# A streaming-encoder step on one core: the down projection's token operands of the fifth pair on are stored and loaded as high and low parts

## The chip, the cores and the metric

One core of one Trainium2 chip runs the whole step as one program. The time is device microseconds (us) of one execution. Five engines work side by side, each on its own instructions in order: TensorE (PE in the profile, with its weight loads listed as PEld), VectorE (DVE), ScalarE (ACT), GpSimd (POOL) and SyncE (SP), whose only work here is to issue the DMAs.

## The reference

The step is one layer of an encoder on 512 prompt frames with 16 meta tokens, and 64 frames of a running stream. After attention comes a SwiGLU feed-forward stage, in which the change lies:

```
h = rmsnorm(x, lp['norm_ffn_g'])
x = x + (jax.nn.silu(h @ lp['ffn_w_gate']) * (h @ lp['ffn_w_up'])) @ lp['ffn_w_down']
...
y_prompt = rmsnorm(xp[:, N_META:], final_norm_g)
y_sample = rmsnorm(xs, final_norm_g)
```

The model width is 2048, `D_FF` is 5632, and 576 tokens pass through this stage. Everything is float32, with an accuracy that one reduced-precision pass does not give.

## The kernel before

**Split operands.** TensorE multiplies in the format fp32r. To keep float32's accuracy each operand is split into a high part (a ScalarE copy into fp32r) and a low part (a VectorE subtraction, source minus high part), and a product is three matmuls: high by high, low by high, high by low. Weights' parts are `wh` and `wl`; the token operands' parts are `bh` and `bl` (pool `bc`).

**Winograd products.** The feed-forward matrices are multiplied in 2 by 2 block form with seven products instead of eight (`winograd`, line 1065). A token operand is one of four quarters (feature chunk `f` by token half, 288 tokens, `QH`) or one of four sums of quarters; a weight operand is a 128 by 128 block or a sum of such blocks. For each product the weight operand is formed (GpSimd or VectorE adds, tile `ws`), split (ScalarE, then VectorE) and multiplied: line 1123 issues `n` times two matmuls with `wh`, line 1127 `n` matmuls with `wl`. `wh` and `wl` have two buffers each, so the weights of a product are split while the one before is multiplied. The matmuls stand in a fixed order; the other engines' orders are the scheduler's, except where `pin` holds them.

**Gate and up.** The 44 chunks of `D_FF` are taken in 22 pairs (`u`, line 1277). Each pair has two turns, gate and up, of seven products with 24 matmuls each (`n` is 8). After the up turn GpSimd multiplies up by the gated value, half by half (line 1312), and forms the four sums of quarters in the gate's tile (lines 1318 to 1321). The product's halves are stored to `actspill` (line 1314) and the sums to `sumspill` (line 1322). These operations run while the next pair's gate turn is multiplied: its products come in the order 1, 2, 4, 5, 6, 3, 7 (`WIDE`).

**Down.** The pairs are consumed in blocks of 4, 4, 4, 4, 4 and 2 (`blocks`, line 1272). For each of the first five blocks there are eight steps `d` (`down_rows`), one for each 256 output columns, of seven products with 12 matmuls each: 84 matmuls a step, products in the order 1, 5, 6, 2, 7, 3, 4 (`CHAIN`). Each adds into the output tiles `y` with a VectorE operation. A step needs 1 MB of `ffn_w_down`, loaded into one of two `raw` buffers, two steps ahead. While one block is multiplied, `builder` (line 1225) makes the token operands of the next block: it loads a quarter or a sum into `bl`, copies it to `bh` on ScalarE and subtracts in place on VectorE, one half-operation for each product of TensorE (`step`, line 1430). The last block (2 pairs) is plain: only quarters, no sums, and its operands are built during the fifth block.

**Queues.** All loads and stores go through SyncE's queue, in its order, with eight completion counters in turn: a DMA waits until the one eight places ahead of it has landed.

Of the kernel before, what the change touches and what calls it, by code (L numbers as in the profile page):

```python
# [11 lines left out]
F32 = mybir.dt.float32  # L12
F32R = mybir.dt.float32r
AF = mybir.ActivationFunctionType
ALU = mybir.AluOpType
# [4 lines left out]
P = 128  # L20
# [8 lines left out]
QH = TQ // 2  # L29
# [6 lines left out]
FC = FF // P  # L36
# [95 lines left out]
def encoder_step(  # L132
# [8 lines left out]
    V, S, Q, G = Engine(tc, nc.vector), Engine(tc, nc.scalar), Engine(tc, nc.sync), nc.gpsimd  # L141
# [4 lines left out]
    dp = ctx.enter_context(tc.tile_pool(name="dp", bufs=1, space=DRAM))  # L146
# [5 lines left out]
    def load(dst, src):  # L152
        Q.dma_start(dst, src)

    def store(dst, src):
        Q.dma_start(dst, src)
# [8 lines left out]
    def f32(ap):  # L165
        return ap.bitcast(F32)
# [151 lines left out]
    x2spill = dp.tile([KC, P, TQ], F32, name="x2spill")  # L318
    actspill = dp.tile([FC, P, TQ], F32, name="actspill")
    sumspill = dp.tile([FC // 2, P, 4, QH], F32, name="sumspill")  # L320
    mspill = dp.tile([KC, P, TQ], F32, name="mspill")
    trow = dp.tile([H, NREL], F32, name="trow")
    tsk = dp.tile([H, P, NREL], F32, name="tsk")
# [6 lines left out]
    with ExitStack() as ph:  # L330
# [33 lines left out]
        with tc.tile_pool(name="xn", bufs=1) as xn, tc.tile_pool(name="xc", bufs=1, side="right") as xc:  # L364
# [3 lines left out]
            for g in (g_attn, g_ffn, g_fin, g_q, g_kv, g_sub):  # L368
                n = g.shape[0] // P
# [123 lines left out]
            for j, (o, n) in enumerate(tok):  # L493
                b = o // TH
# [198 lines left out]
    with ExitStack() as ph:  # L693
# [288 lines left out]
        first = st.spawn(0, latents())  # L982
# [16 lines left out]
    bc, close_bc = pool("bc", "right")  # L999
# [3 lines left out]
    operands = {}  # L1003
    ORDER = (1, 2, 4, 5, 6, 3, 7)
# [9 lines left out]

    pinned = [False]

    def operand(m, p, src):
        hi = bc.tile([P, QH], F32R, name=f"bh{p}_{m}")
        lo = bc.tile([P, QH], F32R, name=f"bl{p}_{m}")
        pin(S.activation(hi, src, AF.Copy))  # L1020
        pin(V.tensor_tensor(lo, src, f32(hi), op=ALU.subtract))
        operands[m, p] = (hi, lo)

    def quarters(b1, b2):
        return b1[:, 0:QH], b1[:, QH:TQ], b2[:, 0:QH], b2[:, QH:TQ]
# [153 lines left out]
    fr, close_fr = pool("fr")  # L1179
# [4 lines left out]
    fb, close_fb = pool("fb", "right")  # L1184


    def stile():
        return fr.tile([P, QH], F32, name="s", tag="s", bufs=4)

    def combined(c11, c12, c21, c22, chain):  # L1190

        s = {}
        copied = {1: c11, 5: c22, 6: c12, 4: c21}
        added = {2: (c11,), 7: (c22,) if chain is CHAIN else (c22, c21), 3: (c12,)}

        def take_sums(p, banks):
            if p in copied:
                S.activation(copied[p], banks[p], AF.Copy)
            else:
                for c in added[p]:  # L1200
                    V.tensor_tensor(c, c, banks[p], op=ALU.add)

        if chain:
            return take_sums

        def take(p, banks):
            if p == 1:
                s[1] = stile()
                S.activation(s[1], banks[1], AF.Copy)
            elif p == 6:  # L1210
                s[2] = stile()
                V.tensor_tensor(s[2], s[1], banks[6], op=ALU.add)
                V.tensor_tensor(c12, s[2], banks[5], op=ALU.add)
            elif p == 3:
                V.tensor_tensor(c12, c12, banks[3], op=ALU.add)
            elif p == 7:
                V.tensor_tensor(s[2], s[2], banks[7], op=ALU.add)
                V.tensor_tensor(c22, s[2], banks[5], op=ALU.add)
                V.tensor_tensor(c21, s[2], banks[4], op=ALU.add)
            elif p == 2:  # L1220
                V.tensor_tensor(c11, s[1], banks[2], op=ALU.add)

        return take

    def builder(m0, count, plain, ahead, by_product=False):

        srcs = {}
        for m in range(m0, m0 + count):
            quarter = [actspill[2 * m + f, :, c] for f in range(2) for c in (slice(0, QH), slice(QH, TQ))]
            if plain:  # L1230
                for p, src in zip((1, 2, 4, 5), quarter):
                    srcs[m, p] = src
            else:
                for p, src in zip(ORDER, (quarter[0], quarter[2], sumspill[m, :, 2], sumspill[m, :, 0],
                                          sumspill[m, :, 1], quarter[3], sumspill[m, :, 3])):
                    srcs[m, p] = src
        order = [p for p, _ in CHAIN]
        todo = sorted(srcs, key=lambda mp: order.index(mp[1])) if by_product else list(srcs)

        def fetch(n):  # L1240
            for m, p in todo[n:n + 1]:
                hi = bc.tile([P, QH], F32R, name=f"bh{p}_{m % 8}")
                lo = bc.tile([P, QH], F32R, name=f"bl{p}_{m % 8}")
                load(f32(lo), srcs[m, p])
                operands[m % 8, p] = (hi, lo)

        for n in range(ahead):
            fetch(n)
        for n, (m, p) in enumerate(todo):
            fetch(n + ahead)  # L1250
            hi, lo = operands[m % 8, p]
            pin(S.activation(hi, f32(lo), AF.Copy))
            yield
            pin(V.tensor_tensor(lo, f32(lo), f32(hi), op=ALU.subtract))
            yield
# [21 lines left out]
    for u in range(FC // 2):  # L1277
        out = {}
        for which, wsrc in (("g", w_gate), ("u", w_up)):
            first = turn == 0  # L1280
            raws = []
            for hf in range(2):
                if turn:
                    rp, bufs = (rw, 1) if turn % 3 == 0 else (fr, 2)
                    raws.append(load_raw(rp, wsrc, hf * 1024, 8, u * 256, bufs))
                turn += 1
            c = fb.tile([P, 2, TQ], F32, name="c", tag="c" + which, bufs=2)
            chain = () if first else CHAIN if u == FC // 2 - 1 and which == "u" else WIDE
            take = combined(*quarters(c[:, 0, :], c[:, 1, :]), chain)
            done = [0]  # L1290

            def step():
                if u == 0 and which == "u":
                    next(norm, None)
                if u == FC // 2 - 1 and which == "u":
                    done[0] += 1
                    if done[0] > 2:
                        for _ in range(2 * blocks[0]):
                            next(start, None)

            if first:
                winograd(fw, fb, raws, range(4, 8), take, banks0, step=step)
            else:
                winograd(fw, fb, raws, range(8), take, step=step, chain=chain)
            out[which] = c
            if u and which == "g":
                gated(c)
        g, w = out["g"], out["u"]
        if u == 0:
            gated(g)  # L1310
        for f in range(2):
            G.tensor_tensor(w[:, f, :], w[:, f, :], g[:, f, :], op=ALU.mult)
            if u < FC // 2 - 1:
                store(actspill[2 * u + f], w[:, f, :])
        if u < FC // 2 - blocks[-1]:
            b11, b12, b21, b22 = quarters(w[:, 0, :], w[:, 1, :])
            t = g.rearrange("p f (h c) -> p (f h) c", h=2)
            G.tensor_tensor(t[:, 0, :], b12, b11, op=ALU.subtract)
            G.tensor_tensor(t[:, 1, :], b22, t[:, 0, :], op=ALU.subtract)
            G.tensor_tensor(t[:, 2, :], b21, t[:, 1, :], op=ALU.subtract)  # L1320
            G.tensor_tensor(t[:, 3, :], b22, b12, op=ALU.subtract)
            store(sumspill[u], t)
    for _ in start:
        pass
    for f in range(2):
# [39 lines left out]

    tok = [[(0, NS), (NS, P), (192, 96)], [(QH, P), (416, P), (544, 32)]]
    sqs = {}

    def squares(i, h):
        c = y[i][:, h * QH:(h + 1) * QH]  # L1370
# [54 lines left out]
    for bi, n in enumerate(blocks):  # L1425
        slots = [(first + k) % 8 for k in range(n)]
        if bi + 1 < len(blocks):
            build = builder(first + n, blocks[bi + 1], bi + 2 == len(blocks), 4)

            def step():  # L1430
                next(build, None)

            for d in range(KC // 2):
                if bi == 0:
                    for i in (2 * d, 2 * d + 1):
                        y.append(yy.tile([P, TQ], F32, name=f"y{i}"))
                        load(y[i], x2spill[i])
                down_rows(first, n, d, slots, step)
            for _ in build:
                pass  # L1440
        else:
            before = iter(())
            for h in range(2):
                for d in range(KC // 2):
                    plain_rows(first, n, d, (h,), slots, squares)
                    if d:
                        for _ in range(2):
                            next(before, None)
                before = finish(h, 5 * h)
            for _ in before:  # L1450
                pass
        first += n
# [78 lines left out]
```

## Time and profile before

| what | value |
| --- | --- |
| median of 3 runs | 2545.82 us (2545.22 to 2546.44) |
| profiled execution, its own time | 2543.0 us |
| its span in the trace | 2541.2 us |
| mean granted TensorE clock | 0.989 |
| gate and up, roughly | 890 to 1970 us of the span |
| down, five Winograd blocks, roughly | 1980 to 2455 us |
| plain block and final norm, roughly | 2455 to 2541 us |

How to read what follows: a view by windows gives, for each stretch of the span, the busy microseconds of PE, PEld, DVE, ACT and POOL with their instruction counts in brackets, then the granted clock, the share of DMA time and the GB/s moved. A timeline row is start, duration, engine, line, operation, output and inputs; in brackets stands the idle time before it and what ended that. Because the helper at line 125 records every operation of VectorE, ScalarE and SyncE, most rows name that line, and the tiles tell what they are. A row of the waits names who waited for whom, the total, the number and the longest. `SPq` rows are DMA issues.

### The profile page before, as it was taken

Reading aid. Unit: us, or ns where it says so; the run is one execution under the profiler, and the core shown is the slowest. Engines: PE = TensorE matmul, PEld = TensorE weight load, DVE = VectorE, ACT = ScalarE, POOL = GpSimd, SP = SyncE. Lnnn points to the kernel's source line nnn. Section 1 sums busy time; section 2 is a strip of 40 time slices with the busy share of each in tenths; the row PEclk is TensorE's granted clock in tenths of the full one; section 3 lists DMA queues with packets and bytes.
Section 4 is the critical chain, followed back from the end, with each engine's and each line's share of the span. In section 5 each row is a group of like instructions: output and inputs, shape, how many; then the busy total and the mean of one; then the engine's idle time right before and its main releaser. Section 6 shows DMA issues by size and latency. Waiting matters only on the chain. (4 is left out here: it accounts for less than half of the span.)

```text
span 2541.2 us, 44865 instructions
## 1 busy us (share of the span) xinstructions
PE 2446.1 (96%) x17847; PEld 2386.6 (94%) x17847; DVE 1799.2 (71%) x2826; ACT 1107.0 (44%) x2008; POOL 739.7 (29%) x614
## 2 busy tenths in 40 slices
PE   7999999989999999999999999999999899999997
PEld 6999999988999888999999999999999799999997
DVE  5555555556555567877777777777777899899975
ACT  5343334334343444444444444444445444444445
POOL 0000000000000164644545445454543222222236
PEclk9999999999999899999999999999999999999999
DMA  7533232334322453333333333333335642452334
GB/s 201 153 86 88 80 85 85 82 97 127 101 89 75 153 155 114 123 133 119 128 99 131 121 123 133 115 120 107 128 128 160 206 156 83 153 161 84 109 102 149
DMA packets 330563, 307.73 MB, mean 121 GB/s; under 512 B 24707, under 2 KB 298506, under 8 KB 330354
## 3 DMA queue, kind: packets, MB, share of 16 engines
q1 hardware_dynamic: 330354, 304.87, 38.3%
q8 instruction: 140, 2.29, 0.4%
q14 instruction: 69, 0.57, 0.1%
HBM read 250.82 MB, written 56.68 MB: 121 GB/s over the span
## 5 line engine op out<-in xcount | busy, mean ns | idle before, releaser
L1123 PE MATMUL m<-bh,wh 128*128 128x288 f32 x3584 | 968.9, 296 | 12.2 <-ACT wh L125 12.2
L1123 PE MATMUL m<-bl,wh 128*128 128x288 f32 x3584 | 968.3, 295 | 0.0
L1123 PEld LDWEIGHTS m<-bh,wh 128*128 128x128 f32 x3584 | 674.3, 188 | 13.2 <-ACT wh L125 13.2
L1123 PEld LDWEIGHTS m<-bl,wh 128*128 128x128 f32 x3584 | 678.1, 189 | 0.1
L1127 PE MATMUL m<-bh,wl 128*128 128x288 f32 x3584 | 585.4, 298 | 17.2 <-DVE wl L125 14.1
L1127 PEld LDWEIGHTS m<-bh,wl 128*128 128x128 f32 x3584 | 512.4, 189 | 30.1 <-DVE wl L125 29.7
L1092 POOL TENSOR_TENSOR ws<-raw 128x512 f32<-128x512 f32 x256 | 343.6, 1350 | 600.1 <-DVE wl L125 344.1
L125 ACT ACTIVATE wh<-ws 128x512 fp32r<-128x512 f32 (+1 forms) x340 | 288.8, 849 | 448.7 <-PE m L1123 293.3
L125 DVE TENSOR_TENSOR wl<-ws,wh 128x512 fp32r<-128x512 f32 (+1 forms) x340 | 379.5, 1116 | 113.7 <-ACT wh L125 113.3
L125 DVE TENSOR_TENSOR wl<-raw,wh 128x512 fp32r<-128x512 f32 x416 | 402.6, 981 | 27.6 <-ACT wh L125 17.4
L125 ACT ACTIVATE wh<-raw 128x512 fp32r<-128x512 f32 x416 | 249.7, 626 | 307.2 <-PE m L1123 274.6
L108 PE MATMUL ps<-xh,wh 128*128 128x296 f32 x960 | 220.8, 311 | 5.2 <-ACT xh L125 3.5
L108 PE MATMUL ps<-xl,wh 128*128 128x296 f32 x960 | 211.0, 301 | 0.9 <-DVE xl L125 0.9
L108 PE MATMUL ps<-xh,wl 128*128 128x296 f32 x960 | 210.8, 301 | 0.2 <-DVE wl L125 0.2
L108 PEld LDWEIGHTS ps<-xh,wh 128*128 128x128 f32 x960 | 157.1, 191 | 9.3 <-ACT xh L125 3.6
L108 PEld LDWEIGHTS ps<-xl,wh 128*128 128x128 f32 x960 | 157.4, 190 | 1.5 <-DVE xl L125 1.5
L108 PEld LDWEIGHTS ps<-xh,wl 128*128 128x128 f32 x960 | 157.2, 190 | 0.9 <-DVE wl L125 0.9
L125 DVE TENSOR_TENSOR y<-y,m 128x288 f32<-128x288 f32 x312 | 139.6, 447 | 25.8 <-PE m L1127 17.6
L125 DVE TENSOR_TENSOR ws<-ws,raw 128x512 f32<-128x512 f32 x128 | 92.3, 722 | 83.9 <-POOL ws L1092 77.5
L125 DVE TENSOR_TENSOR wl<-wr,wh 128x1024 fp32r<-128x1024 f32 (+1 forms) x110 | 117.6, 1070 | 35.3 <-ACT wh L125 33.9
L125 ACT ACTIVATE wh<-wr 128x1024 fp32r<-128x1024 f32 (+1 forms) x110 | 101.6, 928 | 74.1 <-PE ps L108 58.2
L1270 POOL TENSOR_TENSOR c<-c,rb 128x576 f32<-128x576 f32 x44 | 73.0, 1661 | 165.6 <-ACT c L125 165.6
(357 smaller groups left out, 3347.8 us busy)
## 6 DMA issues: line engine op xcount, KB each, us to landing
raw<-in_ffn_w_gate SPq DMA_DIRECT2D x44, 1024.0 KB, 7.0
raw<-in_ffn_w_up SPq DMA_DIRECT2D x44, 1024.0 KB, 5.3
raw<-in_ffn_w_down SPq DMA_DIRECT2D x40, 1024.0 KB, 5.4
wr<-in_w_in SPq DMA_DIRECT2D x60, 512.0 KB, 4.0
actspill<-c SPq DMA_DIRECT2D x44, 288.0 KB, 2.1
sumspill<-c SPq DMA_DIRECT2D x20, 576.0 KB, 3.0
bl<-sumspill SPq DMA_DIRECT2D x80, 144.0 KB, 3.8
bl<-actspill SPq DMA_DIRECT2D x68, 144.0 KB, 3.5
```

What stands on the lines that cost most here:

```text
L108: self.tc.keep_in_program_order(self.pe.matmul(out, lhsT, rhs, start=start, stop=stop))
L125: ins = issue(*args, **kwargs)
L1092: engine.tensor_tensor(w[:, k:k + m, :], pick(xs), pick(ys), op=op)
L1123: PE.matmul(banks[p], wh[:, k, :], x, start=first and new and k == 0 and x is hi, stop=False, skip_group_check=not new)
L1127: PE.matmul(banks[p], wl[:, k, :], hi, start=False, stop=last and k == n - 1, skip_group_check=not new)
L1270: G.tensor_tensor(g[:, f, :], g[:, f, :], rb2, op=ALU.mult)
```

## The change

Operands of pairs 4 to 19 (blocks two to five) are split right after they are made, during gate and up: for each such pair, two ScalarE copies of 128 by 1152 (the product's tile, then the sums' tile) into a tile `hi` with a single buffer, two VectorE subtractions in place, and four stores of 576 KB into `partspill`. The two stores to `actspill` and the one to `sumspill` fall away for these pairs. In the down projection `fetcher` takes `builder`'s place for blocks two to five: one load of 288 KB brings both parts of an operand, and nothing is left to copy or subtract. Blocks one and six are built as before. Both parts of an operand now share one tile, and the scratch tiles of the first gate turn and of the final norm are moved to other pools.

```diff
+    partspill = dp.tile([FC // 2, P, 2, 8, QH], F32, name="partspill")
...
+    def operand_tile(m, p):
+        b = bc.tile([P, 2, QH], F32R, name=f"b{p}_{m}")
+        operands[m, p] = (b[:, 0, :], b[:, 1, :])
+        return b
+
     def operand(m, p, src):
-        hi = bc.tile([P, QH], F32R, name=f"bh{p}_{m}")
-        lo = bc.tile([P, QH], F32R, name=f"bl{p}_{m}")
+        operand_tile(m, p)
+        hi, lo = operands[m, p]
         pin(S.activation(hi, src, AF.Copy))
         pin(V.tensor_tensor(lo, src, f32(hi), op=ALU.subtract))
-        operands[m, p] = (hi, lo)
...
             if p == 1:
-                s[1] = stile()
+                room = fb.tile([P, 4, QH], F32, name="s", tag="hi")
+                s.update({1: room[:, 0, :], 2: room[:, 1, :]})
                 S.activation(s[1], banks[1], AF.Copy)
...
+    def fetcher(m0, count):
+
+        n = 0
+        for m in range(m0, m0 + count):
+            for p in ORDER:
+                q = {1: 0, 2: 2, 3: 3, 5: 4, 6: 5, 4: 6, 7: 7}[p]
+                load(f32(operand_tile(m % 8, p)), partspill[m, :, :, q, :])
+                yield
+                n += 1
+                if n % 2 == 0:
+                    yield
...
         def fetch(n):
             for m, p in todo[n:n + 1]:
-                hi = bc.tile([P, QH], F32R, name=f"bh{p}_{m % 8}")
-                lo = bc.tile([P, QH], F32R, name=f"bl{p}_{m % 8}")
-                load(f32(lo), srcs[m, p])
-                operands[m % 8, p] = (hi, lo)
+                operand_tile(m % 8, p)
+                load(f32(operands[m % 8, p][1]), srcs[m, p])
...
-            if u < FC // 2 - 1:
+            if u < blocks[0] or FC // 2 - blocks[-1] <= u < FC // 2 - 1:
                 store(actspill[2 * u + f], w[:, f, :])
...
-            store(sumspill[u], t)
+            if u < blocks[0]:
+                store(sumspill[u], t)
+            else:
+                for i, src in enumerate((w.rearrange("p f (h c) -> p (f h) c", h=2), t)):
+                    hi = fb.tile([P, 4, QH], F32R, name="hi", tag="hi")
+                    S.activation(hi, src, AF.Copy)
+                    lo = src.bitcast(F32R)
+                    V.tensor_tensor(lo, src, f32(hi), op=ALU.subtract)
+                    store(partspill[u, :, 0, 4 * i:4 * i + 4, :], f32(hi))
+                    store(partspill[u, :, 1, 4 * i:4 * i + 4, :], f32(lo))
...
-            build = builder(first + n, blocks[bi + 1], bi + 2 == len(blocks), 4)
+            if bi + 2 == len(blocks):
+                build = builder(first + n, blocks[bi + 1], True, 4)
+            else:
+                build = fetcher(first + n, blocks[bi + 1])
```

More of the change, by code (lines that the diff above doesn't have):

```diff
@@ L1184, in encoder_step @@
     fb, close_fb = pool("fb", "right")
-    def stile():
-        return fr.tile([P, QH], F32, name="s", tag="s", bufs=4)
     def combined(c11, c12, c21, c22, chain):
@@ L1207, in take @@
             if p == 1:
-                s[1] = stile()
+                room = fb.tile([P, 4, QH], F32, name="s", tag="hi")
+                s.update({1: room[:, 0, :], 2: room[:, 1, :]})
                 S.activation(s[1], banks[1], AF.Copy)
             elif p == 6:
-                s[2] = stile()
                 V.tensor_tensor(s[2], s[1], banks[6], op=ALU.add)
@@ L1367, in encoder_step, with stile @@
     sqs = {}
+    def stile():
+        return yp.tile([P, QH], F32, name="s", tag="s", bufs=4)
     def squares(i, h):
```

## The prediction

> **What bounds the kernel now.** I read the shares of the whole span first, then three windows: the middle of gate and up, the down steps in which the next block's operands are built, and the last down steps, in which they are not.
>
> ```profile
> span 2541.2 us, 44865 instructions
> PE 2446.1 (96%) x17847; PEld 2386.6 (94%) x17847; DVE 1799.2 (71%) x2826; ACT 1107.0 (44%) x2008; POOL 739.7 (29%) x614
> ```
> ```profile
> 1143.00:1460.00 317.00, 317.00 (x2384) 317.00 (x2383) 236.63 (x272) 139.40 (x215) 156.00 (x114) 1.00 0.36 120
> 2000.00:2360.00 360.00, 347.62 (x2535) 337.51 (x2534) 335.02 (x587) 168.84 (x317) 79.92 (x61) 1.00 0.41 131
> 2405.00:2450.00 45.00, 44.87 (x336) 44.47 (x336) 39.33 (x65) 17.72 (x28) 10.35 (x8) 1.00 0.27 83
> ```
>
> In gate and up TensorE never stops: 317 us for 2384 matmuls, 0.1330 us each, with VectorE at 75%. In down with builds it gets 2535 matmuls into 360 us, 0.142 us each, and VectorE is 93% busy. Once the builds are over the rate is 0.134. The clock is 1.00 in all three, so the loss is waiting, and the waits of the down projection say for whom:
>
> ```profile
> PEld m L1127 <- DVE wl L125: 26.1, 49, 1.3
> ACT bh L125 <- DMA bl<-sumspill: 9.1, 4, 5.2
> ```
>
> VectorE is late with `wl`, so it sets the pace there. The length of a down step can be read off GpSimd's first weight sum of each step, from its rows at four steps: 30 steps lie between the first two, 4 between the last two.
>
> ```profile
> 1999.18 1.29 POOL L1092 TENSOR_TENSOR ws<-raw 128x512 f32<-128x512 f32 x1 [6.19 <-DMA raw<-in_ffn_w_down]
> ...
> 2357.89 1.29 POOL L1092 TENSOR_TENSOR ws<-raw 128x512 f32<-128x512 f32 x1 [6.21 <-DMA raw<-in_ffn_w_down]
> ...
> 2394.63 1.71 POOL L1092 TENSOR_TENSOR ws<-raw 128x512 f32<-128x512 f32 x1 [7.09 <-DVE y L125]
> ...
> 2439.64 1.29 POOL L1092 TENSOR_TENSOR ws<-raw 128x512 f32<-128x512 f32 x1 [6.15 <-DMA raw<-in_ffn_w_down]
> ```
>
> With builds a step takes 358.71 / 30 = 11.96 us; without, 45.01 / 4 = 11.25. TensorE alone would need 84 x 0.1330 = 11.17. This kernel thus shows the stage with and without the work that the change takes away.
>
> **Removed from down.** By shape, between 1975 and 2420 us:
>
> ```profile
> L125 DVE TENSOR_TENSOR bl<-bl,bh 128x288 fp32r<-128x288 f32 x124 | 81.5, 659 | 3.0 <-ACT bh L125 3.0
> L125 ACT ACTIVATE bh<-bl 128x288 fp32r<-128x288 f32 x124 | 53.0, 429 | 8.9 <-DMA bl<-sumspill 8.7
> ```
>
> 4 blocks x 4 pairs x 7 operands = 112 subtractions and 112 copies go. At 659 ns the subtractions are 74 us of VectorE, which is not the gain, since TensorE becomes the bound on the way. The gain is the step's: 32 steps (four blocks of eight) from 11.96 to between 11.17 and 11.96. I take 11.35, the measured 11.25 plus 0.1 for the heavier loads (below): 32 x 0.61 = 19.4 us. The best case, 11.17, gives 25.2. The fifth block's steps keep their builder and count nothing.
>
> **Heavier loads.** An operand's load grows from 144 to 288 KB. No arithmetic waits for it any more; TensorE does, a block later. In the changed program's order on SyncE's queue, nine such loads stand between two loads of `raw` in three steps of each block; before, 17 and 11 stood there in two. What a late `raw` holds up is GpSimd's sum, then VectorE's next sum, and behind that in VectorE's order the `wl` of the product after.
>
> ```profile
> raw<-in_ffn_w_down SPq DMA_DIRECT2D x40, 1024.0 KB, 5.4
> sumspill<-c SPq DMA_DIRECT2D x20, 576.0 KB, 3.0
> ```
> ```profile
> 2260.00:2270.00 10.00, 9.53 (x72) 9.29 (x72) 9.56 (x17) 4.54 (x9) 2.59 (x2) 1.00 0.91 293
> ```
> ```profile
> 2180.04 1.28 POOL L1092 TENSOR_TENSOR ws<-raw 128x512 f32<-128x512 f32 x1 [9.02 <-DMA raw<-in_ffn_w_down]
> 2180.30 0.45 ACT L125 ACTIVATE bh<-bl 128x288 fp32r<-128x288 f32 x1 [2.53 <-DMA bl<-sumspill]
> ```
>
> A burst step moves 9 x 295 KB + 1049 KB = 3.70 MB. The burst window moved 293 GB/s at a share of 0.91, so 322 at full share: 11.5 us, against a step of 11.25. The lag is 0.25 us after one such step and 0.75 after three. A normal `raw` lands 5.4 us after issue, about a step and a half ahead of its first product's matmuls, and VectorE now has idle time to catch up. At the measured 293 the lag would be 1.4 us a step, the other bound (a rival below). The second row of the last fence shows a wait that ends outright: ScalarE stood 2.53 us at a load, with weight copies behind it. I take 0.1 us a step.
>
> By the Trainium skill, DMA: Bandwidth & Descriptors, section "Where 436 GB/s comes from", the HBM side gives a core about 358 GB/s; 3.70 MB would then take an estimated 10.3 us and leave no lag, so by the page those 3.2 us (32 x 0.1) come back. No window quoted here reaches 358, so I keep the rows.
>
> **Added to gate and up.** Sixteen pairs get two ScalarE copies and two VectorE subtractions of 1152 columns. The nearest rows, of 1024 columns, with the neighbouring rows that decide where the new ones fit (the pair whose up turn ends near 1255 us):
>
> ```profile
> 1256.04 4.96 DVE L125 TENSOR_TENSOR wl<-raw,wh 128x512 fp32r<-128x512 f32 x4
> 1256.20 1.81 POOL L1312 TENSOR_TENSOR c<-c 128x576 f32<-128x576 f32 x1 [0.45 <-DVE c L125]
> 1257.43 1.16 ACT L125 ACTIVATE wh<-raw 128x512 fp32r<-128x512 f32 x2 [2.04 <-PE m L1123]
> ...
> 1260.41 1.25 POOL L1320 TENSOR_TENSOR c<-c 128x288 f32<-128x288 f32 x1
> 1260.67 1.06 ACT L125 ACTIVATE wh<-ws 128x1024 fp32r<-128x1024 f32 x1 [1.76 <-PE m L1123]
> ...
> 1262.12 1.22 DVE L125 TENSOR_TENSOR wl<-ws,wh 128x1024 fp32r<-128x1024 f32 x1
> 1263.42 2.55 POOL L1092 TENSOR_TENSOR ws<-raw 128x512 f32<-128x512 f32 x2 [1.76 <-DVE wl L125]
> ...
> 1264.96 2.10 DVE L125 TENSOR_TENSOR wl<-ws,wh 128x1024 fp32r<-128x1024 f32 x1 [1.62 <-ACT wh L125]
> ```
> ```profile
> 1260.42 1.24 PE L1127 MATMUL m<-bh,wl 128*128 128x288 f32 x8
> 1263.62 1.24 PE L1127 MATMUL m<-bh,wl 128*128 128x288 f32 x8
> ```
>
> A copy is 1.06 x 1152/1024 = 1.19 us, a subtraction 1.22 x 1152/1024 = 1.37: 2 x 16 x 1.37 = 44 us of VectorE, covered by the 25% in which it idles here, if they fall well. First split: ScalarE's copy waits for GpSimd's second product (end 1258.01), ends 1259.2, and the `wh` copies behind it (1257.43 before) end at 1260.4; TensorE takes up that product 2.13 us (16 x 0.133) before its `wl` at 1263.62, so at 1261.5. ScalarE holds nothing up. The subtraction overwrites the product, so it must wait until GpSimd has read it for the last sum, ending at 1261.66 before. VectorE stands still meanwhile, and behind it stands the `wl` of the third product, due at 1263.62 (first half) and 0.53 later. GpSimd's row of 288 columns takes 1.25 us with VectorE working beside it; in the final norm, with less beside it, the same size takes 0.80:
>
> ```profile
> 2464.14 0.81 POOL L1377 TENSOR_TENSOR s<-s 128x288 f32<-128x288 f32 x1
> ```
>
> With the last three sums at about 0.8 GpSimd ends near 1260.85, the subtraction at 1262.2, the two `wl` at 1262.9 and 1263.5: 0.7 us to spare. With GpSimd's old times it is 1263.0, 1263.7 and 1264.3, a stall of 0.1 to 0.2.
>
> Second split: the copy needs the single `hi` buffer, so the first store (3.0 us to landing) and the subtraction; it runs at about 1262.4 and holds up nothing before 1263.8. Its subtraction meets GpSimd's two `ws` sums, and what is late next is the `wl` of products 6 and 7. The 2.10 us row, against 1.22, shows the price beside GpSimd. I take 0.3 us a pair for all of it, between 0 and 1.3: 16 x 0.3 = +5 us. The stores double, 1152 to 2304 KB a pair; with DMA at 0.36 this costs nothing, and if the cover were gone it would show as a late `raw`.
>
> GpSimd against VectorE is where the Trainium skill speaks against the change: SBUF — State Buffer, section "Who interferes with whom", says a VectorE operation with two SBUF inputs and a GpSimd operation that reads SBUF lock each other out for the whole instruction. The 2.10 and 1.22 us rows agree. With the lock never met, the stall would be 0 and the sum 5 us lower; with it met at both splits, the result is the slower rival.
>
> **The passage into down.** ScalarE's first block is built while loads pile up:
>
> ```profile
> 1970.00:1981.00 11.00, 1.90 (x10) 1.67 (x9) 5.82 (x11) 3.86 (x10) 4.85 (x4) 0.77 0.86 278
> ```
> ```profile
> 1976.24 1.54 ACT L125 ACTIVATE bh<-bl 128x288 fp32r<-128x288 f32 x4 [5.22 <-DMA bl<-sumspill]
> 1978.99 0.63 ACT L125 ACTIVATE wh<-raw 128x512 fp32r<-128x512 f32 x1 [1.20 <-DMA actspill<-c]
> ```
>
> In the old order 13 loads of the second block (144 KB) and one `raw` stand among the first block's 28; in the new one 7 of 288 KB, and the `raw` is behind. That is 880 KB less, 3.2 us at 278 GB/s; but the store that releases ScalarE at 1978.99 depends on GpSimd. The old `y` loads and the heavier loads then meet in the first steps. Between -3 and +3, taken as -1.
>
> Sum: -19.4 + 5 - 1 = -15.4. Against the profiled execution's own 2543.0 us that is 2527.6; the runs' median lies 2.8 higher, so 2530.4.
>
> **The rivals.** *Something else holds down.* `wl` still waits on ScalarE, GpSimd and `raw` in turn, and only half of the 0.71 is won: 32 x 0.35 = 11.4, less 5, plus 1: 2538. Against it stands the 11.25 step with all three present. *Loads eat it.* At 293 GB/s a burst step takes 12.6 us, 1.4 more than 11.25; 112 loads in nines are 12.4 such steps, 17 us. -22.6 + 17 + 5 - 1 = -1.6: 2544, no change. For it speaks the late `raw` at 2180; against it that ScalarE no longer waits there, and that steps without loads recover. *The splits stall gate and up (slower).* If the first subtraction ran beside GpSimd, at 2.10 x 1152/1024 = 2.4 us from 1261.66, the second `wl` would end at 1265.3, 1.1 behind its 1264.15; and the second subtraction locked behind both `ws` sums adds 0.9. That is 2.0 us in each of 16 pairs: +32 - 19.4 - 1 = +11.6, 2557. It decides from 20.4 / 16 = 1.3 us a pair. For it speaks that VectorE waits there in order for GpSimd; against it that GpSimd's next sums themselves wait for VectorE's `wl`, so the first subtraction runs alone.
>
> **How the numbers follow.** The forecast 0.56 (own range 2521 to 2538), something else 0.14, loads 0.12, stalls in gate and up 0.14, others 0.04. A change under 0.2% (5 us) cannot be told from none. Faster: 0.56 + 0.14 + 0.04 of the loads' case = 0.74; same 0.10; slower 0.16. The range runs from 25 us of gain, 2521, to 2549, beyond the loads' case, and leaves out most of the slower one.
>
> **What would show it.** Right: down steps near 11.3 us with few waits of line 1127 for `wl`; no `bh` or `bl` in blocks two to five; TensorE still at 0.133 us a matmul between 1143 and 1460. Wrong: `PEld m L1127 <- DVE wl` growing in gate and up, steps of 12 us where nine loads stand, or 11.6 in all.

## The result and the profile after

The changed kernel takes 2555.46 us (median of 6 runs, 2551.71 to 2556.21) against 2545.52 us for the kernel before (6 runs, 2543.17 to 2546.91): a ratio of 1.0034, with a 95% interval of 1.0024 to 1.0044. It is slower by 0.34%, about 10 us, where 15 us less were forecast. The profiled execution took 2554.93 us; its span follows from the page, with the busy time, the share and the instructions of each engine.

```profile
span 2553.1 us, 44775 instructions
...
PE 2451.6 (96%) x17847; PEld 2390.2 (94%) x17847; DVE 1804.7 (71%) x2746; ACT 1100.9 (43%) x1928; POOL 795.4 (31%) x614
```

GpSimd has the same 614 instructions as before, yet 795.4 us of them instead of 739.7. That is the first trace of what went wrong. The windows of the profile after, in the same columns as the prediction's:

```profile
1143.00:1460.00 317.00, 311.77 (x2320) 308.90 (x2320) 245.32 (x274) 146.76 (x219) 170.04 (x110) 1.00 0.39 134
...
2010.00:2370.00 360.00, 356.71 (x2627) 351.81 (x2627) 308.04 (x502) 138.80 (x220) 82.95 (x63) 0.99 0.60 191
```

Gate and up, where TensorE never stopped, now has 2320 matmuls in 317 us instead of 2384, although the first 68 us of this window lie ahead of the first split (1211 us, below). Down has 2627 in 360 us instead of 2535. The change works where it was meant to, and loses more where its work was moved to.

How much, is read off two kinds of GpSimd rows. Its first product of a pair (`c<-c`, 128 by 576) comes once a pair; these are the fifth pair and the twenty-first, 16 pairs on, in the kernel before:

```profile
1208.06 1.77 POOL L1312 TENSOR_TENSOR c<-c 128x576 f32<-128x576 f32 x1 [3.73 <-DVE c L125]
...
1923.37 1.76 POOL L1312 TENSOR_TENSOR c<-c 128x576 f32<-128x576 f32 x1 [3.75 <-DVE c L125]
```

and in the kernel after:

```profile
1211.14 1.76 POOL L1325 TENSOR_TENSOR c<-c 128x576 f32<-128x576 f32 x1 [3.74 <-DVE c L125]
...
1955.72 1.77 POOL L1325 TENSOR_TENSOR c<-c 128x576 f32<-128x576 f32 x1 [3.69 <-issue]
```

Before, 715.31 us for 16 pairs, 44.71 each; after, 744.58, 46.54 each: 1.83 us more a pair, 29.3 us in all. The first weight sum of a down step, in the kernel after, 30 steps apart:

```profile
2028.69 1.30 POOL L1098 TENSOR_TENSOR ws<-raw 128x512 f32<-128x512 f32 x1 [6.31 <-DMA raw<-in_ffn_w_down]
...
2371.64 1.30 POOL L1098 TENSOR_TENSOR ws<-raw 128x512 f32<-128x512 f32 x1 [6.12 <-DMA raw<-in_ffn_w_down]
```

A step takes 342.95 / 30 = 11.43 us, where it took 11.96: 32 x 0.53 = 17.0 us won.

The whole account of the two spans, 11.9 us apart: 3.1 us were lost before the first split (1211.14 against 1208.06; in the runs below, which do the same work up to there, this row lies between 1208.63 and 1211.42, so single executions differ by as much); 29.3 in the 16 pairs; the rest, from the twenty-first pair's product to the end of the span, fell from 617.83 to 597.38. 3.08 + 29.27 - 20.45 = 11.90.

One pair of the kernel after shows the loss at work. These are rows of the timeline from the end of a gate turn's second product to that of its last (line 1133 is the matmul by `wl`; undisturbed, it comes every 3.19 us; the row at 1453.96 is product 4, the third of the turn, the one at 1468.06 product 7, the last):

```profile
1450.75 1.24 PE L1133 MATMUL m<-b,wl 128*128 128x288 f32 x8
1451.09 0.81 POOL L1333 TENSOR_TENSOR c<-c 128x288 f32<-128x288 f32 x1
...
1451.94 1.36 DVE L125 TENSOR_TENSOR c<-c,hi 128x1152 fp32r<-128x1152 f32 x1 [2.24 <-POOL c L1333]
...
1453.96 1.40 PE L1133 MATMUL m<-b,wl 128*128 128x288 f32 x8
...
1455.92 1.35 DVE L125 TENSOR_TENSOR c<-c,hi 128x1152 fp32r<-128x1152 f32 x1
1456.09 6.82 POOL L1098 TENSOR_TENSOR ws<-raw 128x512 f32<-128x512 f32 x3 [4.18 <-DVE wl L125]
1457.19 4.56 DVE L125 TENSOR_TENSOR wl<-ws,wh 128x1024 fp32r<-128x1024 f32 x2
...
1458.46 0.38 SPq L125 DMA_DIRECT2D raw<-in_ffn_w_up  x1
...
1464.85 1.29 POOL L1098 TENSOR_TENSOR ws<-raw 128x512 f32<-128x512 f32 x1 [1.95 <-DMA raw<-in_ffn_w_up]
...
1468.06 1.33 PE L1133 MATMUL m<-b,wl 128*128 128x288 f32 x8 [0.99 <-DVE wl L125]
```

The two `c<-c,hi` rows are the subtractions. The first stands still for 2.24 us until GpSimd has made the last token sum, but the `wl` of product 4 behind it is hardly late (1453.96 is 3.21 after 1450.75). The second falls just where GpSimd begins its weight sums. These three sums take 6.82 us, and VectorE's two splits beside them 4.56. In the kernel before, the sums of 1263.42 (quoted in the prediction) take 2.55 us for two, and the rows that follow are these:

```profile
1264.74 0.38 SPq L125 DMA_DIRECT2D raw<-in_ffn_w_up  x1
...
1269.90 1.54 POOL L1092 TENSOR_TENSOR ws<-raw 128x512 f32<-128x512 f32 x1 [1.48 <-DMA raw<-in_ffn_w_up]
```

Measured from the `wl` matmul of product 4 (1263.62 before, 1453.96 after), the `raw` buffer is free and its load issued after 1.1 us before and after 4.5 us now; the fourth sum, which waits for that load, begins after 6.3 us before and after 10.9 now. Of these 4.6 us, 2.3 are the later begin of the sums (1456.09 is 2.13 behind product 4's matmul, 1263.42 was 0.20 ahead of it), since they wait for a `wl` that stands behind the first subtraction; 1.05 are the slower first sum (the load is issued 2.37 us after the sums begin, 1.32 before); and 1.2 are the load itself (6.39 us from issue to the fourth sum, 5.16 before). Behind it VectorE's `ws<-ws,raw` is late, and behind that in VectorE's order the `wl` of product 7: TensorE stops for 0.99 us.

All 16 pairs show the same place. Taken between the starts of successive groups of eight of line 1133, the time is 3.19 us everywhere in the kernel before. In the kernel after it is longer, on the mean, by 1.17 us into product 7 of the gate turn (0.64 to 1.49), by 0.24 into product 4 and 0.16 into product 5, and by 0.11 or less elsewhere.

### The profile page after: what moved, and what is told of

Its sections match the earlier page's. It is cut to its first block, busy times and chain, and to the rows that moved or that the text cites. A ratio compares the mean times of both kernels' runs of the same rounds, so it can differ in the third digit from the quotient of the medians.

```text
span 2553.1 us, 44775 instructions
## 1 busy us (share of the span) xinstructions
PE 2451.6 (96%) x17847; PEld 2390.2 (94%) x17847; DVE 1804.7 (71%) x2746; ACT 1100.9 (43%) x1928; POOL 795.4 (31%) x614
## 5 line engine op out<-in xcount | busy, mean ns | idle before, releaser
L1129 PE MATMUL m<-b,wh 128*128 128x288 f32 x7168 | 1048.8, 295 | 10.3 <-DMA b<-partspill 7.5
L1129 PEld LDWEIGHTS m<-b,wh 128*128 128x128 f32 x7168 | 985.6, 189 | 11.3 <-ACT wh L125 11.2
L1133 PE MATMUL m<-b,wl 128*128 128x288 f32 x3584 | 589.3, 299 | 24.0 <-DVE wl L125 22.4
L1098 POOL TENSOR_TENSOR ws<-raw 128x512 f32<-128x512 f32 x256 | 415.9, 1637 | 565.6 <-DVE wl L125 277.8
L1133 PEld LDWEIGHTS m<-b,wl 128*128 128x128 f32 x3584 | 513.0, 189 | 39.0 <-DVE wl L125 35.6
L125 DVE TENSOR_TENSOR wl<-ws,wh 128x512 fp32r<-128x512 f32 (+1 forms) x340 | 408.7, 1206 | 43.9 <-ACT wh L125 43.3
L125 DVE TENSOR_TENSOR wl<-raw,wh 128x512 fp32r<-128x512 f32 x416 | 408.7, 999 | 24.2 <-ACT wh L125 20.5
L1325 POOL TENSOR_TENSOR c<-c 128x576 f32<-128x576 f32 x44 | 78.0, 1772 | 97.6 <-issue 69.3
```

Of the source, the lines that this page charges most:

```text
L125: ins = issue(*args, **kwargs)
L1098: engine.tensor_tensor(w[:, k:k + m, :], pick(xs), pick(ys), op=op)
L1129: PE.matmul(banks[p], wh[:, k, :], x, start=first and new and k == 0 and x is hi, stop=False, skip_group_check=not new)
L1133: PE.matmul(banks[p], wl[:, k, :], hi, start=False, stop=last and k == n - 1, skip_group_check=not new)
```

## The experiments

Three theories were set against each other. **A**: the place of the subtractions in VectorE's order costs the time, through GpSimd's weight sums. **B**: the doubled stores delay the weight loads. **C**: ScalarE's copies, or their single `hi` buffer, hold up the weights. The pair period below is always that of the 16 pairs, from the same two rows as above. A time is that of one run, except in the first two rows (medians of 6), in the row marked 5 runs, and for 2545.99 (the median of 9).

| kernel | us | before, same chip | 5th pair, 21st pair | us a pair |
| --- | --- | --- | --- | --- |
| before | 2545.52 | | 1208.06, 1923.37 | 44.71 |
| changed | 2555.46 | 2545.52 | 1211.14, 1955.72 | 46.54 |
| no subtraction | 2520.72 | 2546.17 | 1208.77, 1925.45 | 44.79 |
| no second subtraction | 2539.12 | 2546.17 | 1211.24, 1939.00 | 45.49 |
| no first subtraction | 2527.95 | 2546.17 | 1211.42, 1929.34 | 44.87 |
| behind product 4, copies free | 2554.76 | 2546.17 | 1210.76, 1955.45 | 46.54 |
| behind product 4, copies too | 2563.88 | 2545.01 | 1210.66, 1965.91 | 47.20 |
| behind product 5 | 2555.56 | 2545.99 | 1210.05, 1956.80 | 46.67 |
| behind product 6 | 2523.92 | 2549.22 | 1209.22, 1925.58 | 44.77 |
| behind product 3 | 2524.12 | 2545.01 | 1209.55, 1925.72 | 44.76 |
| behind product 3, 5 runs | 2526.01 | 2545.99 | 1210.34, 1926.49 | 44.76 |
| behind product 7 | 2528.44 | 2545.99 | 1210.76, 1927.19 | 44.78 |
| on GpSimd | 2579.03 | 2545.01 | 1209.73, 1979.56 | 48.11 |
| half the stores | 2532.63 | 2549.22 | 1208.63, 1935.91 | 45.46 |

(The products of a turn come in the order 1, 2, 4, 5, 6, 3, 7.)

**No subtraction.**

```diff
                     lo = src.bitcast(F32R)
-                    V.tensor_tensor(lo, src, f32(hi), op=ALU.subtract)
```

> Both VectorE subtractions of each split pair are left out (the source is stored as the low part, so the outputs are not the reference's); the two ScalarE copies, the four stores and the loads in down stay. Theory A (the subtractions, through the order of the queues and the time they hold up GpSimd's weight sums): the pair period of gate and up falls from 46.5 us to 44.7-45.0, the end comes 16 x 1.5 to 1.8 = 24 to 29 us earlier, 2526-2531 us. Theory B (the doubled stores delay the weight loads) and theory C (the ScalarE copies and the single hi buffer): the period stays at 46.2-46.6 us, 2550-2556 us.

The period is 44.79, as A said, with all copies and all four stores in place. So B and C fall as causes that act alone. The end came 5 us below A's range; that surplus lies after gate and up, and was not followed up.

**One subtraction at a time.** With `if i == 0:` ahead of the subtraction the second is left out, with `if i == 1:` the first.

> Only the second subtraction (of the sums' tile) is left out; the sums are stored unsplit as low parts, so the outputs are not the reference's. Theory A, with the second subtraction as the main culprit because it runs just ahead of GpSimd's weight sums and of the next weight loads: period 44.9-45.5 us, 2530-2539 us. If the two subtractions cost alike: 45.6 us, about 2540. Theories B and C: 46.2-46.6 us, 2550-2556 us.

> Only the first subtraction (of the product's tile) is left out; the outputs are not the reference's. Theory A with the second as the main culprit: the first holds up one product by about 0.3 us, so the period is 46.0-46.4 us, 2546-2553 us. If the two cost alike: 45.6 us, about 2540. Theories B and C: 46.2-46.6 us, 2550-2556 us.

A's guess at the culprit was wrong: the run without the second fell into its range, at the edge, but the run without the first came in far below all three of its ranges. With the first alone the pair costs 45.49 - 44.71 = 0.78 us more, with the second alone 0.16; together they cost 1.83, or 0.89 more than the two added. The second seems nearly free while VectorE is on time, and dear when the first has made it late. The 0.78 are not the subtraction's alone: in that run ScalarE's second copy also waits for the store that empties `hi`, which it did once, for 1.2 us, in the changed kernel. From its waits between 1215 and 1930 us (who waited for whom, us in total, times, longest):

```profile
ACT hi L125 <- DMA partspill<-hi: 61.9, 16, 4.7
```

**Behind product 4.** The splits of a pair are put on a list; one is taken off in the gate turn after it, one in the up turn, and the subtraction is held at that place in VectorE's order.

```diff
+    def split_parts(u, i, src):
+        hi = fb.tile([P, 4, QH], F32R, name="hi", tag="hi")
+        S.activation(hi, src, AF.Copy)
+        lo = src.bitcast(F32R)
+        tc.keep_in_program_order(V.tensor_tensor(lo, src, f32(hi), op=ALU.subtract))
...
+                if late and done[0] == 3:
+                    split_parts(*late.pop(0))
...
-                    hi = fb.tile([P, 4, QH], F32R, name="hi", tag="hi")
...
+                    late.append((u, i, src))
```

> The same work as the changed kernel, every split kept, but moved in VectorE's order: the first subtraction stands behind the low parts of the fourth weight of the next gate turn, the second behind those of the same weight in the up turn after it, where GpSimd has no sums of the token operands to make. Theory A: period 44.7-45.2 us, 2526-2534 us, faster than both kernels. Theory A', that VectorE's time is short wherever the subtractions stand (2 x 1.35 us a pair): 46 us or more, 2547 us or more. Theories B and C, whose stores and copies are all still there: 46.2-46.6 us, 2550-2556 us.

46.54: nothing is won, so one subtraction a turn is no cure in itself. The waits of the same stretch in this run show a suspect:

```profile
ACT hi L125 <- POOL c L1336: 85.4, 16, 5.5
```

ScalarE's copy, whose place was left to the scheduler, stands up to 5.5 us at the head of its queue waiting for GpSimd's second product. The next runs tell this apart from VectorE's order.

**The place in the turn.** In the next five runs copy and subtraction are both held right behind the split of one product's weights, once in the gate turn and once in the up turn. They differ in the number of that product alone.

```diff
             wh, wl = lhs(p)
+            mid(p)
...
+    def split_parts(u, i, src):
+        hi = fb.tile([P, 4, QH], F32R, name="hi", tag="hi", bufs=1)
+        tc.keep_in_program_order(S.activation(hi, src, AF.Copy))
+        tc.keep_in_program_order(V.tensor_tensor(src.bitcast(F32R), src, f32(hi), op=ALU.subtract))
...
+    def mid(p):
+        if late and p == 3:
+            split_parts(*late.pop(0))
```

> All the work of the changed kernel, in another order: the ScalarE copy and the VectorE subtraction of the first part stand right behind the split of product 3's weights in the next gate turn, those of the second part at the same place of the up turn after it; there VectorE waits 1.2 to 2.5 us for GpSimd's weight sums anyway. If the loss comes from where the subtractions stand in VectorE's order (ahead of the low parts of products 4 to 6, whose end frees the buffers of GpSimd's weight sums): period 44.7-45.2 us, 2521-2531 us. If VectorE's time or its contention with GpSimd is short wherever they stand: 46 us or more, 2547 us or more.

> As the run with the subtractions behind the fourth weight of each turn, but ScalarE's two copies are held back to the same place too, so that no copy waits for GpSimd's second product ahead of a weight copy. If ScalarE's order carried the loss that was left in that run: 44.7-45.2 us, 2521-2531 us. If VectorE's place between products 4 and 5 carries it: only the stall at product 4 goes (0.65 us of a pair), 45.7-46.3 us, 2541-2550 us.

> As the run with the copies and subtractions behind product 3's weights, but both stand right behind the split of product 5's weights in each turn: after the subtraction that frees GpSimd's buffers, ahead of those for products 6 and 3. If what counts is that nothing stands ahead of product 5's low parts: 44.7-45.0 us a pair, 2523-2528 us. If each low part behind the subtraction counts as well (products 6 and 3 come 1.35 us later, and GpSimd's third weight sum with them): 45.2-46.5 us, 2531-2553 us.

> As the runs behind products 4, 5, 3 and 7, but both copies and subtractions stand right behind the split of product 6's weights, so that only product 3's low parts are behind them. If a subtraction is harmful only ahead of a low part whose end frees a buffer for GpSimd's weight sums (products 5 and 6): 44.7-45.2 us, 2522-2531 us. If it is harmful whenever it runs beside those sums: 45.5-46.7 us, 2536-2556 us.

> The same, but behind the split of product 7's weights, ahead of VectorE's own weight sums for product 3 and of the low parts of the next turn's product 1. In the run behind product 3 the low part that product 1 takes ends 1.8 us before TensorE takes it, against 1.35 us for the subtraction. If that room decides: 44.7-45.2 us a pair, 2523-2531 us. If the gating of the gate's result and GpSimd's products, which stand behind in the same order, are held up and come back as stalls in the next turn: 45.5-47 us, 2536-2560 us.

Behind product 3 the loss is gone: 44.76 us a pair with every copy, subtraction and store still there, and 44.76 again in the second profile of the same kernel. This settles that the place, not the amount of the work, costs the time. Behind product 4 with the copies moved too it is 47.20, worse than with the copies free, and beyond both ranges. ScalarE's wait is then mostly gone,

```profile
ACT hi L125 <- POOL c L1339: 19.9, 15, 1.4
```

so it did not carry that run's loss. Why a subtraction here is dearer still than behind product 5 is not shown. The sharpest pair is products 5 and 6: 46.67, just beyond the second range, against 44.77, within the first. These are the rows behind product 5:

```profile
1405.65 1.24 PE L1134 MATMUL m<-b,wl 128*128 128x288 f32 x8
...
1406.91 1.34 DVE L125 TENSOR_TENSOR c<-c,hi 128x1152 fp32r<-128x1152 f32 x1
...
1407.06 6.81 POOL L1098 TENSOR_TENSOR ws<-raw 128x512 f32<-128x512 f32 x3 [1.16 <-DVE wl L125]
1408.17 4.54 DVE L125 TENSOR_TENSOR wl<-ws,wh 128x1024 fp32r<-128x1024 f32 x2
...
1409.43 0.37 SPq L125 DMA_DIRECT2D raw<-in_ffn_w_up  x1
...
1415.90 1.29 POOL L1098 TENSOR_TENSOR ws<-raw 128x512 f32<-128x512 f32 x1 [2.02 <-DMA raw<-in_ffn_w_up]
...
1419.10 1.33 PE L1134 MATMUL m<-b,wl 128*128 128x288 f32 x8 [0.52 <-DVE wl L125]
```

and these behind product 6, in the same turn (the first PE row of each is product 4's matmul by `wl`):

```profile
1398.78 2.55 POOL L1098 TENSOR_TENSOR ws<-raw 128x512 f32<-128x512 f32 x2 [1.16 <-DVE wl L125]
1398.89 1.24 PE L1134 MATMUL m<-b,wl 128*128 128x288 f32 x8
...
1400.10 0.38 SPq L125 DMA_DIRECT2D raw<-in_ffn_w_up  x1
...
1400.23 2.18 DVE L125 TENSOR_TENSOR wl<-ws,wh 128x1024 fp32r<-128x1024 f32 x1 [1.53 <-ACT wh L125]
...
1402.33 1.35 DVE L125 TENSOR_TENSOR c<-c,hi 128x1152 fp32r<-128x1152 f32 x1
1402.49 2.33 POOL L1098 TENSOR_TENSOR ws<-raw 128x512 f32<-128x512 f32 x1 [1.16 <-DVE wl L125]
...
1406.56 1.29 POOL L1098 TENSOR_TENSOR ws<-raw 128x512 f32<-128x512 f32 x1 [1.74 <-DMA raw<-in_ffn_w_up]
```

In the good order VectorE stands still between the `wl` of products 5 and 6 (1.53 us, waiting for ScalarE). GpSimd makes its first sum in that gap and two sums in 2.55 us; it is VectorE's `wl` that is stretched by the second (2.18 us), and that is not late. A subtraction behind product 5 fills the gap; the sums then run beside VectorE's own work, three in 6.81 us, and the first frees its buffer, so that the load is issued, 2.4 us after the sums begin instead of 1.3. The fourth sum begins 8.8 us after the first instead of 7.8. The load takes as long in both, 6.5 us from issue to that sum. The sums also begin later against product 4's matmul, 1.4 us behind it instead of 0.1 ahead, because VectorE comes late out of the turn before, which had a subtraction at the same place (TensorE waits 0.29 us for its `wl` at 1395.56). TensorE then waits 0.52 us for the `wl` of product 7. An idle gap of VectorE was of use: it was GpSimd's time. The waits of the whole stretch, 1215 to 1930 us, agree. In the kernel before:

```profile
DVE wl L125 <- ACT wh L125: 92.3, 80, 1.7
...
DVE ws L125 <- POOL ws L1092: 41.1, 32, 2.4
```

and after:

```profile
DVE ws L125 <- POOL ws L1098: 98.2, 61, 2.9
...
DVE wl L125 <- ACT wh L125: 22.6, 45, 1.0
PEld m L1133 <- DVE wl L125: 22.3, 26, 1.6
```

and with the splits behind product 3 (the timed run below):

```profile
DVE wl L125 <- ACT wh L125: 93.9, 79, 2.0
...
DVE ws L125 <- POOL ws L1098: 3.8, 3, 1.4
```

VectorE's waits for ScalarE went from 92.3 to 22.6 us and came back with the cure. What the subtraction fills there is VectorE's wait for GpSimd, 41.1 us before and 3.8 then. A row in which TensorE's weight loads wait for `wl` is missing in the kernel before and in the cured one. Behind product 6, where the period is as good, VectorE's waits for ScalarE come back only to 56.2 us, so their total is a sign of the cause and not a measure of the loss.

Behind product 7 the period is as good (44.78). The room read off the run behind product 3, 1.8 us, sufficed; the feared return in the next turn did not come.

**On GpSimd.** The same list, with the subtraction given to GpSimd behind product 7's weights.

```diff
+        tc.keep_in_program_order(G.tensor_tensor(src, src, f32(hi), op=ALU.subtract))
...
+        if late and p == 7:
```

> The two subtractions run on GpSimd, behind its last weight sum of the gate turn and of the up turn, where it waits 5.6 us (for the gate's SiLU) and 3.7 us (for the product's operands) in the trace of the changed kernel; ScalarE's copies stand at the same places. Twice GpSimd's 1.8 us for 128 by 576 is 3.6 us each. If these idle times cover them: 44.7-45.2 us, 2521-2531 us. If a GpSimd operation with two SBUF inputs holds up VectorE (or is held up) as long as it runs: the low parts of products 1 and 2, which VectorE makes in that time, come late, 46 us or more, 2547 us or more.

48.11, the worst of all, though GpSimd is idle there. The rows say why:

```profile
1469.22 2.68 POOL L1291 TENSOR_TENSOR c<-c,hi 128x1152 f32<-128x1152 f32 x1
1469.31 3.15 DVE L125 TENSOR_TENSOR ws<-ws,raw 128x512 f32<-128x512 f32 x1 [2.31 <-POOL ws L1098]
...
1473.65 1.34 PE L1134 MATMUL m<-b,wl 128*128 128x288 f32 x8 [1.66 <-DVE wl L125]
```

VectorE's sum began 0.09 us after GpSimd's subtraction and ended only after it: 3.15 us, where it takes 0.69 alone. Behind it the `wl` of product 7 was late, and TensorE stood 1.66 us.

**Half the stores.**

```diff
                     store(partspill[u, :, 0, 4 * i:4 * i + 4, :], f32(hi))
-                    store(partspill[u, :, 1, 4 * i:4 * i + 4, :], f32(lo))
...
-                load(f32(operand_tile(m % 8, p)), partspill[m, :, :, q, :])
+                load(f32(operand_tile(m % 8, p)), partspill[m, :, 0, min(q, 6):min(q, 6) + 2, :])
```

> The changed kernel without the two stores of low parts of each pair (1.15 MB of the 2.3 MB that it stores in a pair; before stored 1.15 MB); down loads two neighbouring high parts instead, as many bytes, so the outputs are not the reference's. Copies and subtractions stay where they are. If the stores take no part: the period stays at 46.3-46.6 us, 2550-2556 us. If the doubled stores, by delaying the weight loads whose landing GpSimd's fourth sum waits for, carry a part of the loss: 45.0-46.2 us, 2530-2549 us.

45.46: with the subtractions where they were, the stores carry 46.54 - 45.46 = 1.08 of the 1.83 us. B was thus half right. The rows of one gate turn of this run:

```profile
1450.07 6.82 POOL L1098 TENSOR_TENSOR ws<-raw 128x512 f32<-128x512 f32 x3 [4.17 <-DVE wl L125]
...
1452.44 0.38 SPq L125 DMA_DIRECT2D raw<-in_ffn_w_up  x1
...
1457.62 1.29 POOL L1098 TENSOR_TENSOR ws<-raw 128x512 f32<-128x512 f32 x1 [0.74 <-DMA raw<-in_ffn_w_up]
...
1460.88 1.28 PE L1133 MATMUL m<-b,wl 128*128 128x288 f32 x8
```

The sums are as slow as in the changed kernel (6.82 us) and the load is issued as long after they begin (2.37 us in both), but the fourth sum starts 5.2 us after that issue instead of 6.4 (1464.85 - 1458.46), and TensorE does not stop at product 7. Over the 16 pairs the time into product 7 of the gate turn is now longer by only 0.07 us on the mean, instead of 1.17, so what the stores carry is nearly all of that one stall. The 1.2 us of a load are decisive only because the sums had used up the room: with the splits behind product 3 all four stores cost nothing. In the rows shown the delay lies behind the load's issue. Whether the load is slowed by sharing the DMA engines with the stores, or by its place among them in SyncE's queue, was not tried apart.

**The better order, timed.** The kernel with the splits behind product 3 again.

> The kernel of the run behind product 3 again, for its time: 2524 us against the kernel before's 2545.5, a ratio of 0.9916 with an interval of at most 0.002 to either side. If that run was a chance: 2530 us or more.

2526.01 us (5 runs, 2524.13 to 2526.82) against 2545.99 (9 runs, 2542.57 to 2547.53): a ratio of 0.9924, interval 0.9910 to 0.9937, so 0.76% faster than the kernel before, and some 1.2% faster than the changed one (2526.01 / 2555.46 = 0.988, from two sets of runs). The 0.9916 expected lies inside the interval; the median is 2 us above the one expected. Its window of gate and up has TensorE busy throughout, with as many matmuls as before the change:

```profile
1143.00:1460.00 317.00, 317.00 (x2384) 317.00 (x2384) 260.05 (x284) 149.56 (x224) 160.27 (x113) 1.00 0.41 138
```

## Why the prediction was wrong

**Down, right.** The step was to fall from 11.96 to 11.35 us and fell to 11.43; the term was 19.4 us and is 17.0. TensorE's weight loads wait 7.3 us for `wl` between 2010 and 2370 us, where they waited 21.6. The heavier loads did not undo it, though they nearly fill the DMA engines. A window of the kernel after, where nine loads stand in a step:

```profile
2200.00:2220.00 20.00, 20.00 (x151) 19.77 (x150) 18.78 (x30) 7.59 (x12) 5.09 (x4) 1.00 0.99 315
```

315 GB/s at a share of 0.99 is close to the rate that the prediction took from the burst window (322 at full share), and TensorE is busy all through it. So *Loads eat it* falls. The 358 GB/s that the Trainium skill gives (DMA: Bandwidth & Descriptors, section "Where 436 GB/s comes from") were not reached in this window; keeping the row was right.

**The passage, inside its range.** -1 was taken, between -3 and +3. From the twenty-first pair's product to the first of the rows that gave the step it is 75.81 us before (1999.18 - 1923.37) and 72.97 after (2028.69 - 1955.72), two down steps included: -2.84. Down and passage together were to give -20.4, and all that follows that product gave -20.45. This near a match is luck: the steps gave 2.4 us less than forecast, and the passage and what lies behind the steps as much more.

**The first split, right in kind.** ScalarE's copy held up nothing. VectorE stood 2.24 us for GpSimd's last sum, which took the 0.81 us assumed, and the matmuls by the third product's `wl` began 0.02 us late (1453.96 - 1450.75 - 3.19) and took 1.40 us instead of 1.24: the 0.1 to 0.2 us that were named. On the mean of the 16 pairs it is more, 0.24 into product 4 and 0.16 into product 5. (The prediction's 1260.85 needs only the last two sums at 0.8, not three; they did take 0.81 each.) What follows from this wait was not named: all of VectorE's work behind it comes later against GpSimd's.

**The step that failed** is "I take 0.3 us a pair for all of it, between 0 and 1.3: 16 x 0.3 = +5 us". It is 1.83 us a pair and 29.3 us, beyond the upper bound, and 1.17 of the 1.83 lie at product 7 of the gate turn. The place was named ("what is late next is the `wl` of products 6 and 7"), and the 2.10 us row was quoted as the price. Two things were missed. One was that the price is paid by GpSimd as well: its sums begin 2.3 us later in the pair shown and go from 1.33 to 1.92 us each on the mean, and this delays not one `wl` but a chain (buffer free, load, fourth sum, VectorE's next sum, `wl` of product 7). The prediction wrote this very chain down for down and did not apply it to gate and up. These groups of GpSimd's between 1215 and 1930 us, with busy time and mean ns, are before

```profile
L1092 POOL TENSOR_TENSOR ws<-raw 128x512 f32<-128x512 f32 x128 | 169.5, 1334 | 162.6 <-DVE wl L125 109.7 <-DMA raw<-in_ffn_w_gate 27.0 <-DMA raw<-in_ffn_w_up 25.9
```

and after:

```profile
L1098 POOL TENSOR_TENSOR ws<-raw 128x512 f32<-128x512 f32 x124 | 235.5, 1919 | 144.2 <-DVE wl L125 98.8 <-DMA raw<-in_ffn_w_up 32.0 <-DMA raw<-in_ffn_w_gate 8.2
```

The other was "with DMA at 0.36 this costs nothing", said of the stores: it is 1.08 us a pair as long as the sums are late, and nothing once they are not. The sentence behind it, that a lost cover "would show as a late `raw`", holds in the single rows (6.4 us from issue to fourth sum after, 1269.90 - 1264.74 = 5.2 before), not in GpSimd's total wait for the two loads (40.2 us after, 52.9 before), because sums that start late find their load further on.

**The rivals.** *The splits stall gate and up* came true, at 2557 forecast and 2555.46 measured, with 2.0 us a pair forecast and 1.83 measured. Its mechanism was only half the real one, so that its number is so near is luck: 1.1 of its 2.0 us came from a first subtraction slowed by GpSimd. The first subtraction did run alone (1.36 us, not 2.4), as the objection to the rival said; what the objection overlooked is that GpSimd's sums, by waiting for VectorE's `wl`, come to lie beside the second subtraction and the `wl` behind it. The rule of the Trainium skill that was quoted against the change (SBUF — State Buffer, section "Who interferes with whom") agrees with the GpSimd run, 0.69 us becoming 3.15 beside 2.68. By itself it does not give the time: the two met in the run behind product 6 too (a sum of 2.33 us, a `wl` of 2.18), and cost nothing there.

The error, then, lay in pricing "covered by the 25% in which it idles": that idle time is worth what it is only at some places, and the place was the scheduler's choice.

## What to carry to other kernels

Idle time of one engine can be another engine's working time where the two get in each other's way, so before filling a gap look at who runs in it; here the gap behind product 5 was taken and the one behind product 6, 3 or 7 was free. When work is added to an engine off the critical path, follow what its queue releases (buffers, then loads, then sums) up to the bound engine, and let each delay be added to the next, since single costs do not add (0.78 + 0.16 against 1.83). If a change wins in one stage and loses in another, first hold the added instructions at other places of the order: the same work cost from 0.05 to 2.5 us a pair.

## What the runs showed of the hardware

How long VectorE and GpSimd hold each other up was not expected: a VectorE sum of 128 by 512 took 0.69 us alone and 3.15 us when begun 0.09 us after a GpSimd subtraction of 2.68. Side by side for longer, with the end of a subtraction ahead of them, three GpSimd sums took 6.82 us and two VectorE splits 4.56, against 1.29 and 1.22 us apiece alone, 3.9 and 2.4 in all. GpSimd's 1152 columns took less than was estimated from its 576-column row: 2.68 us instead of 2 x 1.8.
